# A two-layer decoder trunk on one core: the order of every engine's instructions found with the tile context's other machine model

## The chip, the cores and the metric

The kernel runs on one core of a Trainium2 chip. A core has a matrix engine (TensorE, PE in the profile), three engines for elementwise work (VectorE or DVE, ScalarE or ACT, GpSimd or POOL), a queue engine that here only issues DMAs (SyncE, SP), an on-chip memory (SBUF) and accumulator banks behind the matrix engine (PSUM). The metric is the device time of one execution in microseconds (us), the median of several.

## The reference, cut to what matters

The reference is a trunk of two layers for one sequence of 512 tokens with 1024 features, in fp32. Its loop is

```python
for layer in range(DEPTH):
    g = norm_gains[layer]
    hn = rmsnorm(x, g[0])
    if layer % 2 == 0:
        mix = fox_gdn_mixer(hn, ...)        # forgetting attention (8 heads) | gated DeltaNet (4 heads)
    else:
        mix = hgrn2_mamba2_mixer(hn, ...)   # HGRN2 (4 heads) | Mamba-2 SSD (8 heads)
    x = x + rmsnorm(mix, g[1])
    hn = rmsnorm(x, g[2])
    x = x + rmsnorm(conv_ffn(hn, ...), g[3])
```

Each mixer is one input projection, two kinds of heads side by side, and an output projection. The conv-FFN is an up projection to 2 x 2816 columns, a short causal convolution over the tokens, silu(gate) * up, and a down projection. The recurrences (DeltaNet, HGRN2, SSD) are computed in chunks of 64 or 128 tokens: scores within a chunk, and a state that is carried from chunk to chunk by a scan. The DeltaNet also solves a triangular system in each chunk. The HGRN2 scores need, per feature, products of decays between two tokens.

## The kernel before, in words

All large products are made of three fp32r matmuls: each operand is split into a high and a low part, and hi*hi, hi*lo and lo*hi are summed in PSUM. A weight block is loaded by SP into a tile raw (L183), ACT casts the high part (hi, L186) and DVE subtracts it for the low part (lo, L187). The products have three helpers: feature-major blocks fm (L247 to L249), token-major groups tm (L301 to L303), and the output projections y (L321 to L323). One such matmul has 512 columns; the text calls it a large one. They use four PSUM banks (psA). Everything else on PE, the "side" matmuls of the heads, takes its bank from four others (psB).

Layer 0's mixer has, beside the large products, the attention heads (up to L533) and the DeltaNet: pm (L626) makes the matrices M of the chunks, M goes through DRAM (stored at L630 as dM, loaded at L660 as Ms) into a layout in which DVE inverts blocks of 16 by 15 pairs of small instructions (L671, L672; base16), the results go back through DRAM as dX and dY (L673, L676, loaded at L680, L682), three doubling steps finish the solve (pp L698, pq L705, px L712), and the scan over four chunks follows. A step of the scan is pks (L725) on PE, r on DVE, pu (L731) on PE, u on ACT, pst (L738) on PE and the new state S on DVE; po and pqs (L749, L756) make its output, and pt (L395) transposes it.

Layer 1's mixer runs, beside the large products, four HGRN2 heads. A head (hgrn_head) first makes raw scores pdq (L888), which ACT copies into acc (L890) and POOL masks (L891):

```python
S.copy(A, pdq)
G.tensor_tensor(v4(A), v4(A), bcm(ident, 4), op=ALU.mult)
```

Then it goes through seven block sizes. For each of the first six, DVE subtracts the first halves of a tile Z (L904) and POOL the second halves (L905), ACT takes the exponential (L906), DVE and POOL multiply the halves by k and q (L907, L908), PE makes the products pz (L916) and DVE copies a part of them into acc (L922). The seventh needs one POOL product (L911). POOL also makes el, qg and kd of a head (L927, L930, L934), and PE pk (L938). After the SSD's small columns (L383) a softplus on DVE ends in `a` (L968), and three small matmuls pg (L970 to L972) sum it. The convolution of the SSD's input is four taps on a tile cv, the first on ACT (L343), three on DVE (L345). The SSD block then makes per chunk masks W on DVE (L1020), their products pd (L1021), pcb (L1028, L1029), an exponential, a POOL product LT (L1034), px, pst and py (L1038, L1051, L1062). The scans of HGRN2 (L1097 to L1110) and the transposes for the output projection (L395) follow.

What sets the order: the program's text names, by generators and a table PACE, in which order the instructions are emitted, large products and side streams interleaved. This order is only a priority. At the exit of the tile context a list scheduler plays the whole program on a model of the machine and places, on each engine, at each moment the ready instruction that comes first in priority; tiles wait for free buffers of their pools. What the model says about durations so decides what stands next to what. The kernel is compiled with the order found, and each engine then runs its list strictly in order. The context is opened at the end of the host function:

```python
with tile.TileContext(nc) as tc:
    trunk(tc, *args)
```

Of the kernel before, what the change touches and what calls it, by code (L numbers as in the profile page):

```python
# [16 lines left out]
P = 128  # L17
T = 512
NT = T // P
D = 1024  # L20
# [7 lines left out]
# rounds of the side streams per block of the products they run beside  # L28
PACE = dict(heads=(3, 3, 4, 2), ssd=(0, 2, 1), scan=5, gate=1, fox=(3, 4, 3), pre=2, pre_from=4, base=8, at=8, solve=(1, 1), small=4)
# rows of blocks by which the first token tile of a group runs ahead, and the row before which the other group's norms stand  # L30
LEAD = (3, 3)
NORMS = (1, 4)
# columns of the packed per-feature constants
C_GCONV, C_MCONV, C_MCB, C_FCONV, C_FCB, C_LBL, C_END = 0, 48, 80, 88, 352, 440, 448
# columns of the packed rows
R_FB, R_DTB, R_GAL, R_MDT, R_MAL, R_MD, R_GG, R_HG, R_MG, R_END = 0, 8, 12, 16, 24, 32, 40, 168, 296, 808
# columns of the shape constants
# [4 lines left out]
def trunk(ctx: ExitStack, tc: tile.TileContext, x, gains, w_s, w_a, w_b, w_o, w_u, w_d, gcols, cols, rows, consts, out, taps=None):  # L42
    nc = tc.nc
# [43 lines left out]
    def bc3(col, n, w):  # L87
        """[P, n] -> [P, n, w], each column spread over w"""
        return col.unsqueeze(2).to_broadcast([P, n, w])

    def bcm(m, n):
        """[P, w] -> [P, n, w], the same for each n"""
        return m.unsqueeze(1).to_broadcast([P, n, m.shape[1]])
# [34 lines left out]
    def rsq(out_, in_, n):  # L128
        """out = in ** -0.5"""
        G.tensor_tensor(out_, in_, negh[:, :n], op=ALU.pow)  # L130
# [3 lines left out]
    # 16 matrices [128, 128] each, 128 apart: their 128 diagonal 16 x 16 blocks are evenly spaced  # L134
# [5 lines left out]
    def chunk4(d, n):  # L140
        """[128 rows, 4 matrices, 128 columns] of chunk n"""
# [3 lines left out]
    def diag16(d):  # L145
        """[128, 16, 16]: the 16 x 16 diagonal blocks"""
# [12 lines left out]
    def lockstep(gens):  # L159
        """all advance by one step per round"""  # L160
# [5 lines left out]
    def skewed(gens):  # L166
        """one more starts per round"""
# [29 lines left out]
    def inv_rms(src):  # L197
        """1 / rms of the token tile src (two halves)"""
# [6 lines left out]
        r = tn(1, "r")  # L205
# [3 lines left out]
    def prenorm(t, xt, which, hT, bank):  # L209
        """rmsnorm of the token tile xt (two halves), transposed into hT columns of tile t"""  # L210
# [21 lines left out]
    def postnorm(xt, y, gain):  # L232
        """xt += rmsnorm(y) * gain; y: two banks"""
# [17 lines left out]
    def fm_small(ps, src, hT):  # L251
        """as fm_mm, for up to 16 features: src [128, 8 * 48] holds them twice, from columns 0 and 32.
        Rows 0 of the bank get the products with the weights' upper parts, rows 32 those with the rest."""
# [14 lines left out]
    def fm_blocks(srcs, hT, done, nsplit=0):  # L268
        """feature-major products: one [128 features, 512 tokens] bank each, handed to done(i, bank).
        The first nsplit blocks take the last token tile separately."""  # L270
# [19 lines left out]
    def tm_group(srcs, hT, done, meanwhile=None):  # L290
        """token-major product: 512 features for all the tokens; done(t, bank). meanwhile() after every quarter"""
# [19 lines left out]
    def out_group(srcs, lhs, bank, hooks, lead):  # L311
        """two token tiles times [K, 1024]: lhs(k) -> per token tile (hi, lo); returns banks[tile][half].
        The first tile takes the last lead rows of blocks before the second one does. hooks[k]() before row k"""
# [26 lines left out]
    def conv(ps, taps_, bias, width, slot=slot):  # L340
        """causal depthwise conv along the free axis: taps_ [P, width]; -> slot"""
# [6 lines left out]
    def silu_half(out_, yh, slot=slot):  # L348
        """out = silu(2 yh), by tanh"""
# [4 lines left out]
    def softplus(xs, n, tagp):  # L354
        """softplus of [P, n] (max(x, 0) + log1p(exp(-|x|)), the latter as 2 atanh(u / (2 + u)))"""
# [21 lines left out]
    def small_cols(ps, n, slot=slot):  # L377
        """bank of fm_small -> [128, 4, n] (tokens on partitions)"""
# [12 lines left out]
    def to_mx(src, slot=slot):  # L391
        """token-major [128 tokens, 512] -> split transposed [128, 4, 128]"""
# [7 lines left out]
    # ================= layer 0: FoX | gated DeltaNet =================  # L400
    def mixer0(hT):
        # FoX projections
        # q: its upper part in the rows of its head, the rest in the other head's rows; k: the upper part in both, and the rest
# [44 lines left out]
        # per-token scalars  # L448
# [19 lines left out]
        # -8 * cumsum(log_f), as rows spread over the partitions  # L468
# [892 lines left out]
```

## Time and profile before

| what | value |
|---|---|
| time, median of 3 runs | 1393.02 us (1390.69 to 1393.9) |
| span of the profiled execution, first to last instruction | 1391.2 us |
| the profiled execution's own time | not listed apart from the three above; the median is 1.8 us over its span |
| PE busy | 1343.0 us, 97% of the span, 6836 matmuls |
| DVE, ACT, POOL busy | 893.7 (64%), 664.0 (48%), 151.6 us (11%) |
| mean granted clock of PE | 0.993 of full speed |

The profile is one execution taken by the hardware profiler. A matmul counts as busy from its start to its modelled end, so PE's busy share says where it had work, not that the work ran at its peak. Where an engine was idle, the profile names the instruction that ended the wait. [...]

### The profile page before, as it was taken

How to read it: one execution, taken by the hardware profiler on the slowest of the kernel's cores; microseconds unless marked ns; L12 is line 12 of the kernel's file. 1: busy time of each engine (PE TensorE's matmuls, PEld its weight loads, DVE VectorE, ACT ScalarE, POOL GpSimd, SP SyncE). 2: the span in 40 equal slices, each digit the busy share in tenths (PEclk: the TensorE clock that was granted, in tenths of full speed). 3: DMA queues.
4: the chain of work that ended last, by engine and by line, in shares of the span. 5: the costliest groups of instructions: out<-in, count | busy, mean ns of one | idle time of the engine just before them, and what ended most of it. 6: DMA issues, size and time to landing. Idle time of an engine off the chain costs nothing. (4 is left out here: it accounts for less than half of the span.)

```text
span 1391.2 us, 18400 instructions
## 1 busy us (share of the span) xinstructions
PE 1343.0 (97%) x6836; PEld 1124.6 (81%) x6836; DVE 893.7 (64%) x1616; ACT 664.0 (48%) x1253; POOL 151.6 (11%) x159
## 2 busy tenths in 40 slices
PE   7999999999999999999999879899999999999998
PEld 6877777887988888888888768678888888888886
DVE  5546777667865565556664877876677556555564
ACT  6625644435744434346554534425575443434552
POOL 0000111101000000000010546452010000000000
PEclk9999999999999999999999989999999999999999
DMA  6341123315433333266653212111544323334663
GB/s 227 112 139 59 46 76 61 102 46 176 152 98 105 91 100 98 92 177 201 207 186 97 61 46 77 46 40 55 195 137 123 106 91 100 97 92 149 193 223 117
DMA packets 59418, 159.82 MB, mean 115 GB/s; under 512 B 11968, under 2 KB 18624, under 8 KB 59328
## 3 DMA queue, kind: packets, MB, share of 16 engines
q1 hardware_dynamic: 57600, 156.44, 36.1%
q10 hardware_dynamic: 1728, 2.20, 0.4%
q8 instruction: 54, 0.88, 0.3%
q14 instruction: 36, 0.29, 0.1%
HBM read 151.00 MB, written 7.62 MB: 114 GB/s over the span
## 5 line engine op out<-in xcount | busy, mean ns | idle before, releaser
L187 DVE TENSOR_TENSOR lo<-raw,hi 128x1024 fp32r<-128x1024 f32 x264 | 323.8, 1230 | 333.1 <-ACT hi L186 332.7
L186 ACT CAST hi<-raw 128x1024 fp32r<-128x1024 f32 x264 | 276.6, 1052 | 320.2 <-PE fm L248 130.2
L247 PE MATMUL fm<-hh,hi 128*128 128x512 f32 (+1 forms) x1120 | 411.7, 369 | 2.0 <-ACT hh L229 1.6
L249 PE MATMUL fm<-hh,lo 128*128 128x512 f32 (+1 forms) x1120 | 411.8, 368 | 0.0
L248 PE MATMUL fm<-hl,hi 128*128 128x512 f32 (+1 forms) x1120 | 411.3, 368 | 0.0
L247 PEld LDWEIGHTS fm<-hh,hi 128*128 128x128 f32 x1120 | 212.3, 190 | 37.1 <-ACT hh L229 2.0
L249 PEld LDWEIGHTS fm<-hh,lo 128*128 128x128 f32 x1120 | 212.6, 190 | 34.8 <-issue 1.2
L248 PEld LDWEIGHTS fm<-hl,hi 128*128 128x128 f32 x1120 | 212.6, 190 | 34.5 <-issue 1.4
L321 PE MATMUL y<-hi,ahl 128*128 128x512 f32 x352 | 137.2, 390 | 0.0
L322 PE MATMUL y<-lo,ahl 128*128 128x512 f32 x352 | 136.9, 389 | 0.0
L323 PE MATMUL y<-hi,ahl 128*128 128x512 f32 x352 | 136.6, 389 | 0.0
L345 DVE SCALAR_TENSOR_TENSOR cv<-fm,col,cv 128x511 f32<-128x511 f32 (+1 forms) x176 | 130.8, 746 | 2.8
L130 POOL TENSOR_TENSOR r<-ms,negh 128x1 f32<-128x1 f32 x32 | 21.1, 664 | 820.3 <-DVE ms L204 820.3
L321 PEld LDWEIGHTS y<-hi,ahl 128*128 128x128 f32 x352 | 66.1, 188 | 14.1 <-issue 0.5
L323 PEld LDWEIGHTS y<-hi,ahl 128*128 128x128 f32 x352 | 66.1, 188 | 13.9
L322 PEld LDWEIGHTS y<-lo,ahl 128*128 128x128 f32 x352 | 66.1, 188 | 13.6
L191 ACT CAST ahl<-cv 128x256 fp32r<-128x256 f32 x88 | 34.6, 404 | 83.7 <-DVE cv L1244 83.7
L1240 ACT ACTIVATE cv<-cv 128x512 f32<-128x512 f32 x44 | 27.8, 632 | 84.8 <-DVE cv L345 84.8
L343 ACT ACTIVATE cv<-fm,col 128x512 f32<-128x512 f32 x88 | 68.1, 774 | 0.0
L301 PE MATMUL tm<-hi,hh 128*128 128x512 f32 x160 | 63.8, 398 | 4.4 <-DVE cv L345 4.4
L303 PE MATMUL tm<-hi,hl 128*128 128x512 f32 x160 | 62.9, 395 | 0.0
L302 PE MATMUL tm<-lo,hh 128*128 128x512 f32 x160 | 62.8, 392 | 0.0
(325 smaller groups left out, 1727.0 us busy)
## 6 DMA issues: line engine op xcount, KB each, us to landing
raw<-in_w_u SPq DMA_DIRECT2D x88, 512.0 KB, 3.6
raw<-in_w_d SPq DMA_DIRECT2D x88, 512.0 KB, 4.2
raw<-in_w_o SPq DMA_DIRECT2D x32, 512.0 KB, 3.7
raw<-in_w_a SPq DMA_DIRECT2D x28, 512.0 KB, 3.6
raw<-in_w_b SPq DMA_DIRECT2D x28, 512.0 KB, 3.7
x<-in_x SPq DMA_DIRECT2D x16, 256.0 KB, 4.7
g<-in_gains SPq DMA_DIRECT2D x4, 512.0 KB, 4.5
xs_dram<-x SPq DMA_DIRECT2D x8, 256.0 KB, 2.9
```

Source lines behind the costliest of these rows:

```text
L186: S.copy(hi, raw)
L187: V.tensor_tensor(lo, raw, hi.bitcast(F32), op=ALU.subtract)
L247: PE.matmul(ps[:, a:b], lhsT=wh, rhs=hh[:, a:b], start=(k == 0), stop=False)
L248: PE.matmul(ps[:, a:b], lhsT=wh, rhs=hl[:, a:b], start=False, stop=False)
L249: PE.matmul(ps[:, a:b], lhsT=wl, rhs=hh[:, a:b], start=False, stop=(k == KB - 1))
L301: PE.matmul(banks[t], lhsT=hh[:, a:b], rhs=wh, start=(k == 0), stop=False)
L303: PE.matmul(banks[t], lhsT=hl[:, a:b], rhs=wh, start=False, stop=(k == KB - 1))
L321: PE.matmul(y[j][half], lhsT=ah, rhs=hi[:, c], start=(k == 0), stop=False)
L322: PE.matmul(y[j][half], lhsT=ah, rhs=lo[:, c], start=False, stop=False)
L323: PE.matmul(y[j][half], lhsT=al, rhs=hi[:, c], start=False, stop=(k == n - 1))
L343: S.activation(y, ps, AF.Identity, bias=bias if bias is not None else 0.0, scale=taps_[:, width - 1:width])
L345: V.scalar_tensor_tensor(y[:, s_:], ps[:, :T - s_], taps_[:, width - 1 - s_:width - s_], y[:, s_:], ALU.mult, ALU.add)
```

## The change: the scheduler's machine model

One argument is added where the tile context is opened, so that the scheduler plays the program on the other model that the context offers. The rest of the difference is comments and text strings in functions that were taken out; no instruction is added or taken away on any engine, except that one of ACT's six table loads stands at another line (L925 in place of L906).

```diff
     args.append(nc.dram_tensor("out_0", (T, D), F32, kind="ExternalOutput").ap())
-    with tile.TileContext(nc) as tc:
+    with tile.TileContext(nc, schedule_with_timeline_sim=True) as tc:
         trunk(tc, *args)
```

What moves is the order. In the conv-FFNs it is the same on all engines. It differs in layer 0's mixer (from some 100 to 380 us of the trace of before), in layer 1's mixer and output projection (720 to 1060 us), and by a few rows at the start, the boundaries of the layers and the end. Counted over the program, 2922 rows of difference are on PE, 1412 on DVE, 769 on ACT, 108 on POOL and 84 on SP. Three places follow. A name is a tile and its number, then what it is made from; x4 means four in a row.

On PE, around pg (L970) in layer 1, before; tm are large matmuls of the tokens' products, pz_7389 is the second block size of the second head:

```order
L301 MATMUL tm_7419<-hi_7487,hh_5446 128x512
L302 MATMUL tm_7419<-lo_7488,hh_5446 128x512
L303 MATMUL tm_7419<-hi_7487,hl_5447 128x512
L970 MATMUL pg_7373<-a_7371,kc 128x32
L971 MATMUL pg_7373<-a_7371,kc 128x32
L972 MATMUL pg_7373<-a_7371,kc 128x32
L916 MATMUL pz_7389<-Z_7383 128x128 x4
L916 MATMUL pz_7401<-Z_7395 128x128 x4
```

And the same place in the changed kernel:

```order
L302 MATMUL tm_7419<-lo_7609,hh_5454 128x512
L303 MATMUL tm_7419<-hi_7608,hl_5455 128x512
L301 MATMUL tm_7420<-hi_7608,hh_5454 128x512
L970 MATMUL pg_7373<-a_7371,kc 128x32
L971 MATMUL pg_7373<-a_7371,kc 128x32
L972 MATMUL pg_7373<-a_7371,kc 128x32
L916 MATMUL pz_7389<-Z_7383 128x128 x4
L916 MATMUL pz_7401<-Z_7395 128x128 x4
```

The rows of pg stand behind other large matmuls: the weight hi_7608 is two further on than hi_7487. Counted, 49 more large matmuls stand ahead of pg, and 41 more ahead of the first pz of the first head (pz_7080).

On POOL, the second head of HGRN2, a piece of the difference (- is before, + is the changed kernel); Z_7299, Z_7383 and so on are the block sizes from 64 down, acc_7296 the head's scores:

```order
 L905 TENSOR_TENSOR Z_7299<-G_7014 128x4x64
-L891 TENSOR_TENSOR acc_7296<-acc_7296,kc 128x512
 L905 TENSOR_TENSOR Z_7383<-G_7014 128x8x32
 L905 TENSOR_TENSOR Z_7395<-G_7014 128x16x16
-L908 TENSOR_TENSOR Z_7299<-Z_7299,sg_6833 128x4x64
-L908 TENSOR_TENSOR Z_7383<-Z_7383,sg_6833 128x8x32
 L905 TENSOR_TENSOR Z_7407<-G_7014 128x32x8
 L905 TENSOR_TENSOR Z_7453<-G_7014 128x64x4
 L905 TENSOR_TENSOR Z_7465<-G_7014 128x128x2
 L911 TENSOR_TENSOR Z_7477<-sg_6860,sg_6833 128x512
+L891 TENSOR_TENSOR acc_7296<-acc_7296,kc 128x512
+L927 COPY el_7517<-eg_7515 128x4
```

The mask of the scores (L891) moved from the second place of the head behind all its subtractions (L905) and L911. Heads 1 and 4 have the same move; in head 3 it stands behind three of the six subtractions.

On PE, the scan of the gated DeltaNet in layer 0, from the first pst (L738) on, before; y are large matmuls of the output projection:

```order
L738 MATMUL pst_2968<-u_2963,kd_1503 128x128 x4
L321 MATMUL y_3214<-hi_3218,mxh_2702 128x512
L322 MATMUL y_3214<-lo_3219,mxh_2702 128x512
L323 MATMUL y_3214<-hi_3218,mxl_2703 128x512
L321 MATMUL y_3215<-hi_3218,mxh_2702 128x512
L725 MATMUL pks_2975<-S_2973,qkv_976 128x128
L725 MATMUL pks_2975<-S_2973,qkv_1063 128x128
L725 MATMUL pks_2975<-S_2973,qkv_1171 128x128
L725 MATMUL pks_2975<-S_2973,qkv_1269 128x128
L322 MATMUL y_3215<-lo_3219,mxh_2702 128x512
L323 MATMUL y_3215<-hi_3218,mxl_2703 128x512
L321 MATMUL y_3212<-hi_3236,mxh_2628 128x512
```

And in the changed kernel:

```order
L738 MATMUL pst_2968<-u_2963,kd_1503 128x128 x4
L725 MATMUL pks_2975<-S_2973,qkv_976 128x128
L725 MATMUL pks_2975<-S_2973,qkv_1063 128x128
L725 MATMUL pks_2975<-S_2973,qkv_1171 128x128
L725 MATMUL pks_2975<-S_2973,qkv_1269 128x128
L731 MATMUL pu_2985<-r_2980,Y_2480 128x128 x4
L738 MATMUL pst_2995<-u_2990,kd_1539 128x128
L749 MATMUL po_3005<-u_2963,ET_1723 128x128 x4
L738 MATMUL pst_2995<-u_2990,kd_1539 128x128 x3
L725 MATMUL pks_3030<-S_3000,qkv_976 128x128
L725 MATMUL pks_3030<-S_3000,qkv_1063 128x128
```

The large matmuls that stood between the scan's steps are gone from there: between the first pu and the first pt behind the scan stand 44 large matmuls before and 11 in the changed kernel, all 11 ahead of the first pst.

## Rows read from the trace of the kernel before

**Rows 1.** The page's part 1: busy time, share of the span and instructions of each engine.

```profile
PE 1343.0 (97%) x6836; PEld 1124.6 (81%) x6836; DVE 893.7 (64%) x1616; ACT 664.0 (48%) x1253; POOL 151.6 (11%) x159
```

**Rows 2.** Stretches: from:to, length, busy us of each engine, clock, DMA share, GB/s.

```profile
210.00:280.00 70.00, 65.40 (x428) 56.90 (x427) 48.36 (x116) 28.62 (x76) 9.15 (x8) 1.00 0.32 81
...
420.00:490.00 70.00, 70.00 (x310) 57.98 (x309) 42.08 (x53) 28.38 (x40) 0.00 (x0) 1.00 0.32 98
...
770.00:840.00 70.00, 57.55 (x303) 48.08 (x302) 57.29 (x87) 26.87 (x43) 37.11 (x40) 0.90 0.17 53
840.00:910.00 70.00, 62.99 (x344) 52.90 (x343) 57.79 (x113) 27.69 (x42) 30.77 (x31) 1.00 0.21 61
910.00:980.00 70.00, 66.29 (x384) 56.28 (x383) 51.08 (x103) 32.91 (x87) 30.39 (x26) 1.00 0.16 50
```

**Rows 3.** Waits of PE: line, what it waited for, us in total, times, longest.

```profile
PE pg L970 <- DVE a L968: 6.8, 1, 6.8
PE pz L916 <- POOL Z L908: 4.4, 2, 3.9
PE tm L301 <- DVE cv L345: 4.4, 2, 3.1
...
PE pd L1021 <- DVE W L1020: 2.5, 3, 1.6
```

**Rows 4.** Timeline of PE: start, us, instruction [idle before, what ended it].

```profile
775.95 2.62 PE L916 MATMUL pz<-Z 128*128 128x128 f32 x16 [3.94 <-POOL Z L908]
...
821.43 0.64 PE L970 MATMUL pg<-a,kc 128*128 128x32 f32 x2 [6.81 <-DVE a L968]
...
956.82 0.90 PE L395 MATMUL pt<-kc,y 128*128 128x128 f32 x4 [1.45 <-DVE y L1086]
```

**Rows 5.** Stretches at the lower clock, columns as in rows 2.

```profile
777.26:780.68 3.42, 3.42 (x13) 2.94 (x12) 3.42 (x5) 2.88 (x5) 3.42 (x5) 0.50 0.00 0
...
821.43:828.46 7.03, 7.03 (x33) 7.03 (x34) 1.28 (x4) 0.45 (x2) 0.00 (x0) 0.50 0.21 72
```

**Rows 6.** Timeline of DVE, the instruction that makes `a`.

```profile
821.19 0.19 DVE L968 SCALAR_TENSOR_TENSOR a<-spl,ea 128x32 f32<-128x32 f32 x1
```

**Rows 7.** Waits of POOL.

```profile
POOL acc L891 <- ACT acc L890: 36.3, 3, 16.1
```

**Rows 8.** Timelines of PE and of DVE, the SSD block.

```profile
900.12 0.39 PE L1021 MATMUL pd<-W,sLR 128*128 128x512 f32 x1
...
918.90 0.78 PE L1062 MATMUL py<-X,LT 128*128 128x64 f32 x6
...
894.68 0.84 DVE L1020 TENSOR_SCALAR W<-kc,ahi 128x128 fp32r<-128x128 f32 x4
...
901.79 2.95 DVE L1020 TENSOR_SCALAR W<-kc,ahi 128x128 fp32r<-128x128 f32 x4
```

**Rows 9.** Timeline of PE, layer 0: pm, pp, pu, pt.

```profile
203.62 1.11 PE L626 MATMUL pm<-qkv 128*128 128x128 f32 x8
...
243.83 1.16 PE L698 MATMUL pp<-Y,M 128*128 128x128 f32 x8 [1.58 <-DMA Y<-dY]
...
284.70 1.06 PE L731 MATMUL pu<-vb,Y 128*128 128x128 f32 x8
...
312.86 1.02 PE L395 MATMUL pt<-kc,gg 128*128 128x128 f32 x4 [0.85 <-DVE gg L770]
```

**Rows 10.** Load of Ms on SP, its landing, DVE's first instruction on it.

```profile
208.64 0.36 SPq L660 DMA_DIRECT2D Ms<-dM  x1
...
Ms<-dM SPq DMA_DIRECT2D x1, 128.0 KB, 3.1
...
214.31 0.07 DVE L661 MEMSET Ms<- 128x16 f32 x1
```

**Rows 11.** DVE L904: all by form, and two places of the timeline.

```profile
L904 DVE TENSOR_TENSOR Z<-G 128x256 f32<-128x256 f32 x24 | 20.9, 902 | 0.0
...
848.02 1.09 DVE L904 TENSOR_TENSOR Z<-G 128x256 f32<-128x256 f32 x3
...
866.02 1.46 DVE L904 TENSOR_TENSOR Z<-G 128x256 f32<-128x256 f32 x1
```

## The prediction

> **What bounds the kernel now.** I read the page's busy table first: TensorE (PE) is busy 1343.0 of 1391.2 us, the next engine, VectorE (DVE), 64% [rows 1]. So the end is set by PE, and since the change leaves every instruction on its engine, the time can only move by what PE does not do: idle time and time at the lower clock. The table by 70 us stretches shows where these are. Inside a conv-FFN PE is busy 70.00 of 70 with 310 matmuls, 0.226 us for each large one; short of 70 are 210 to 280 (65.40), 770 to 840 (57.55, mean clock 0.90), 840 to 910 (62.99) and 910 to 980 (66.29) [rows 2]. The first is layer 0's mixer, the other three are layer 1's. The waits say what ended the idle time: one of 6.8 us for `a` (L968), 4.4 us for POOL's Z (L908), 4.4 for the convolution's first tap (L345), 2.5 for W (L1020) [rows 3]. [...]
>
> **What the change moves.** Nothing is added or removed but the place of one table load on ACT. In the two conv-FFNs the order is the same on every engine; at the start, the boundaries and the end matmuls move by a few rows, where PE is busy nearly all the time. I give these parts 0, bounds -1.5 and +1.5. What is left are five places, each costed as: large matmuls that now stand ahead of a point, times 0.226 us, against the time at which its input can be there.
>
> **1. From the first pz to pg (layer 1): -11.** 41 more large matmuls (9.3 us) stand ahead of the first pz, more than its wait of 3.94 [rows 4], so that wait goes. Ahead of pg (L970) stand 49 more, 11.1 us. pg now starts at 821.43, 0.05 us after the instruction that makes `a` ends [rows 4, 6]. The DVE work in front of `a` is nearly the same, and DVE is busy 57.29 of the 70 us [rows 2]; of the 12.7 others 5.75 lie in the 7.03 us behind pg's start [rows 5]. So `a` comes at about the same time, and PE has by then done 11.1 us more. Without a long idle time the half clock behind pg (3.5) goes as well: 14.6 at most. Against it: on DVE the copy of the first pz's result (L922) now stands behind a tap of a convolution, and the third pz must wait for that PSUM bank. Walking both orders with the trace's durations I get a wait of 4 us there and pg at 824 instead of 821.4, and I leave 1 us for a clock that falls after that wait: 14.6 - 2.6 - 1 = 11. Bounds: 7 (`a` 7.6 us later or the clock lost again) and 14.6.
>
> **2. From pg to the last pz: -5.** POOL's mask of the scores (L891) waits for ACT's copy of the same head's pdq. Now it stands second or third in a head's POOL work, and POOL waited there three times, 36.3 us together [rows 7], with five of the six subtractions (L905) or more queued behind it. In the new order of heads 1, 2 and 4 all six and L911 stand ahead of it, in head 3 three of the six. PE's idle time between 840 and 910 is 70 - 62.99 = 7.0 [rows 2], of which some 6 lie before the last pz and are waits for Z or a tap behind Z. I take 5 of them; bounds 0 (DVE's half of Z is late as well) and 6.
>
> **3. The SSD block: +5.** Between the fourth pd (L1021) and the first py (L1062) stand 41 large matmuls now and none after: they are spent earlier, on places 1 and 2. The stretch takes 18.8 us now (900.12 to 918.90) [rows 8]; 41 x 0.226 = 9.3 of it are those matmuls, some 2.5 waits for W [rows 3], so 7 are its own matmuls. What feeds them is a chain: W on DVE, pd, exp, POOL's product, py. The block needs 32 W: at the price of 4 in 0.84 us that is 6.7 us, at 2.95 for 4 (while POOL works) 23.6 [rows 8]. With the other DVE work of the chain I walk 13.5 us, so 6.5 of idle time in place of 2.5: +4, and +1 for the next stretch up to the scan's first pst. Bounds 0 and +9 (18.8 again, less the waits already there, less 7).
>
> **4. The output projection's start: -1.4.** 22 more large matmuls (5 us) stand ahead of the transpose at 956.82 that waits 1.45 us now [rows 4]. Bounds -1.5 and 0.
>
> **5. Gated DeltaNet in layer 0: +4.** Three stretches [rows 9]. From pm (203.62) to the solve's first pp (243.83), 40.2 us, the number of large matmuls falls from 96 to 72, 5.4 us less cover; now 3.9 of the 40.2 are not matmuls, so 36.3 - 5.4 = 30.9 remain. The chain there (pm, M, store, load, base16, store, load) can shrink: the load of Ms was issued at 208.64 and took 3.1, but DVE only came to clear its tile at 214.31 [rows 10], held by a weight's L187 that the new order puts behind; and no weight load stands between the stores of dX and dY on SP any more. I take 36, so 5 us of stall in place of 3.9: +1. From pp to pu (284.70), 40.9 us, 20 large matmuls more (4.5 us) cover small waits: -1.5. From pu to pt (312.86), 28.2 us, the scan keeps 11 of its 44: 33 x 0.226 = 7.5 us less. Its matmuls alone take 28.2 - 2.2 - 7.5 = 18.5; the chain pst, S, pks, r, pu, u cannot run in less than that nor should it need more than 28.2. I take 25, near the upper end, since each of three steps crosses to DVE and ACT and back: 6.5 of stall for 2.2, +4.3. Sum +4; bounds -5 (chains as short as the matmuls: -3.9 - 1.5, nearly all of the idle time now) and +11.5 (both chains as long as now: stalls of 9.3 and 9.7 for 3.9 and 2.2, less 1.5).
>
> **Sum.** -11 - 5 + 5 - 1.4 + 4 = -8.4. Since the walk is by hand I round toward no change: -8. The durations come from one execution with a span of 1391.2 us; its own time isn't among the three shown, whose median is 1393.02, 1.8 above that span. I subtract from the median: 1385.0.
>
> [...] DVE's first half of Z (L904) took 0.36 us each when three ran while POOL waited (848.02, 1.09 for 3), 1.46 for one while POOL worked (866.02), and 902 ns in the mean of 24 [rows 11]. [...]
>
> **The rivals.**
> *Larger gain.* Places 3 and 5 cost nothing, because what feeds them is also earlier: -11 - 5 - 1.4 - 1.5 (pp to pu) = -19: 1374. For it: pz's last matmul would then come some 17 us earlier than now, and DVE isn't busy all the time behind it. Against it: 41 matmuls fewer beside W, 33 fewer beside the scan.
> *No change: DVE sets layer 1's stage.* If all 24 L904 ran at 1.46 instead of 0.902, DVE would need 13.4 us more; if half of that lands ahead of `a` and of the last pz, places 1 and 2 fall from -16 to -9, and with +5, -1.4 and +4 about -1.5 is left: 1391.5, at most 1395. For it: rows 11 and DVE's 57 us of 70. Against it: POOL's work is the same, only less interrupted.
> *Slower: the scan and solve of layer 0 run bare.* If both chains of place 5 stay as long as now, the stage loses 11.5 more than now, and one fall of the clock like that behind pg adds 3.5, together 15. With places 1 to 4 as forecast (-12.4) this gives +2.6: 1395.6; with places 1 and 2 at their low ends (-7, 0) it gives -7 + 5 - 1.4 + 15 = +11.6: 1404.6; between the two, 1400. For it: the order leaves the scan 11 large matmuls. Against it: DVE and SP have less in front of base16. It decides when the stage from 200 to 320 loses more than layer 1 gains: from 12.4 us on with places 1 to 4 as forecast.
>
> **How the numbers follow.** The three times of before span 3.2 us, so 0.2% (2.8 us, below 1390.2 or above 1395.8) is about what can be told from no change. Forecast 0.50 (its own range 1378 to 1390), larger gain 0.14, no change 0.16, slower 0.20. The forecast's upper edge lies at the bound, so nearly all of it counts as faster: faster 0.62, with a little of the forecast in the same: same 0.18, slower 0.20. The range leaves out half of the larger gain and rather more than half of the slower case: 1372 to 1398.
>
> **What would show each step.** In the changed profile: place 1 right if pg waits under 2 us and no half clock follows, wrong if pg's wait is again over 5 us, or starts after 830. Place 2: POOL's wait at L891 far below 36 us, PE's idle time in the heads under 3 us. Place 3: waits of py or pd for W, LT or the like of 6 to 8 us in a row where there were 2.5. Place 5: waits of pks, pu or pst in the scan of some 6 us and of pp for the DMA of 4 to 5. It is wrong as a whole if DVE's mean of L904 rises above 1.2 us with pg late, or if the stage of layer 0 loses over 12 us.

## The result, and the profile after

The changed kernel took 1412.9 us, the median of 4 runs (1409.97 to 1415.96), beside 1393.33 for the kernel before on the same chip: a ratio of 1.0151, 95% interval 1.0131 to 1.0172. It is slower by 1.5%, some 20 us, where 8 us faster was forecast. The profiled execution took 1409.97 us with a span of 1408.2. It is compared below with the profiled span of before, 1391.2: 17.0 us to explain.

The busy table, beside [rows 1]:

```profile
PE 1351.3 (96%) x6836; PEld 1136.3 (81%) x6836; DVE 896.4 (64%) x1616; ACT 663.4 (47%) x1253; POOL 151.2 (11%) x159
```

PE has the same 6836 matmuls and is busy 8.3 us longer, so about half of the loss is no idle time. The table by 70 us stretches (columns as in [rows 2]) shows why: three of six stretches have a mean granted clock below 1.00, which is full speed; in before it was one of these six (770 to 840, 0.90).

```profile
140.00:210.00 70.00, 66.08 (x324) 52.40 (x324) 37.32 (x157) 36.77 (x116) 9.18 (x8) 0.88 0.14 42
210.00:280.00 70.00, 65.94 (x413) 56.14 (x412) 52.40 (x154) 28.44 (x81) 6.61 (x6) 1.00 0.34 89
280.00:350.00 70.00, 62.38 (x400) 54.86 (x399) 43.16 (x94) 28.55 (x83) 10.40 (x9) 1.00 0.19 59
...
770.00:840.00 70.00, 59.80 (x299) 49.19 (x299) 55.95 (x69) 31.48 (x48) 38.93 (x37) 0.95 0.20 62
840.00:910.00 70.00, 65.58 (x381) 56.77 (x380) 59.99 (x106) 27.46 (x43) 30.37 (x31) 1.00 0.21 62
910.00:980.00 70.00, 61.19 (x340) 52.80 (x339) 45.84 (x113) 24.84 (x69) 31.05 (x26) 0.93 0.12 38
```

The waits of PE, beside [rows 3]:

```profile
PE pz L916 <- DVE acc L922: 10.0, 2, 8.3
PE pd L1021 <- DVE W L1020: 8.0, 4, 3.9
...
PE tm L301 <- DVE cv L345: 3.8, 2, 2.2
PE pt L395 <- DVE gg L770: 2.6, 1, 2.6
...
PE pu L731 <- DVE r L728: 2.0, 3, 1.1
...
PE pt L520 <- ACT s L516: 1.4, 2, 1.1
```

The wait of pg for `a` and that of pz for POOL's Z are gone, as forecast. A wait of pz for its bank (8.3) and the waits for W (8.0) have taken their place. The timeline of PE at the points of [rows 4] and [rows 9]:

```profile
223.53 0.33 PE L626 MATMUL pm<-qkv 128*128 128x128 f32 x1
...
257.57 0.27 PE L698 MATMUL pp<-Y,M 128*128 128x128 f32 x1
...
302.07 0.28 PE L731 MATMUL pu<-vb,Y 128*128 128x128 f32 x1
...
331.56 0.30 PE L395 MATMUL pt<-kc,gg 128*128 128x128 f32 x1 [2.57 <-DVE gg L770]
...
815.34 2.05 PE L916 MATMUL pz<-Z 128*128 128x128 f32 x8 [8.35 <-DVE acc L922]
...
850.36 0.30 PE L970 MATMUL pg<-a,kc 128*128 128x32 f32 x2
```

How a loss is read from such starts: pm begins 19.9 us later than in [rows 9] (223.53 against 203.62). 37 large matmuls more stand ahead of it, 37 x 0.226 = 8.4 us of work that isn't lost but done earlier. So 11.5 us are lost by then. The same sum at each point gives this account, where a place's loss is the difference between the sums at its two ends; both a lower clock and idle time are in it. "Small" stands from here on for PE's side matmuls, though some of them have 512 columns too.

| place | forecast | loss (+) or gain (-) |
|---|---|---|
| start, attention heads, up to pm of layer 0 | 0 | +11.5 |
| 5: pm to pu | -0.5 | -1.6 |
| 5: the scan, pu to pt | +4.3 | +8.8 |
| pt to layer 1's first pdq | 0 | +1.7 |
| 1: first pdq to pg, with the half clock behind pg | -11 | -6.1 |
| 2: pg to the last pz, without that half clock | -5 | -1.6 |
| 3: SSD block, to the scan's pst | +5 | +10.5 |
| 4: output projection's start | -1.4 | -1.6 |
| output projection and boundary behind it | 0 | -4.9 |
| sum (in the prediction -8.4, with place 5 rounded) | -8.6 | +16.7 |

Two of the smaller rows hold a half clock that one trace has and the other lacks. The first of these two stretches, all at 0.50, is from after: its 3.42 us of matmuls at half speed cost 1.7, the +1.7 of the fourth row. The second is from before and is in the -4.9 (number 12).

```profile
371.22:374.64 3.42, 3.42 (x17) 3.42 (x18) 3.42 (x9) 2.29 (x8) 0.54 (x1) 0.50 0.99 311
...
1012.78:1016.19 3.41, 3.41 (x15) 2.92 (x14) 2.62 (x7) 1.25 (x4) 0.00 (x0) 0.50 0.74 229
```

The largest term is at a place that the prediction gave 0 without looking into it. All of it is lost behind the twelfth of the attention's 32 scores (L504; 157.43 in after, 135.27 in before): up to there the sum is -0.2. The stretches from this score to pm (columns as in [rows 2]):

```profile
157.43:166.43 9.00, 7.89 (x44) 5.49 (x42) 5.18 (x24) 4.85 (x13) 1.27 (x1) 1.00 0.20 58
166.43:183.49 17.06, 16.04 (x54) 12.87 (x54) 11.36 (x53) 9.87 (x39) 3.30 (x3) 0.50 0.01 1
183.49:223.53 40.04, 37.47 (x212) 29.61 (x210) 24.48 (x95) 22.03 (x65) 4.58 (x4) 1.00 0.15 46
```

For 17.06 us the granted clock stood at 0.50, and PE was busy 16.04 of them: at half speed these cost 8.0 us. Idle times, the longest 1.11 us, make 4.7 more. Together that is a little over the 11.5, so the split is an estimate. In before, the same attention work, from its twelfth score to pm, ran at the full clock throughout:

```profile
134.90:203.60 68.70, 68.52 (x370) 53.10 (x369) 47.89 (x188) 40.53 (x124) 9.19 (x8) 1.00 0.18 55
```

Counted by their starts, 136 of the 367 matmuls between the two points are large in before and 74 of 305 in the changed kernel; the 231 small ones are the same. From 157.43 to 183.49, where the clock fell, 11 large ones start, 9 of them at its end. What PE did just before the fall, in its timeline:

```profile
163.33 0.42 PE L504 MATMUL ps<-fqk,fqk 128*128 128x384 f32 x1
163.69 0.44 PE L505 MATMUL ps<-fkl,fqk 64*128 64x384 f32 x1
165.23 0.72 PE L520 MATMUL pt<-kc,s 128*128 128x128 f32 x3 [1.11 <-ACT s L516]
165.71 0.48 PE L504 MATMUL ps<-fqk,fqk 128*128 128x512 f32 x1
166.12 0.55 PE L505 MATMUL ps<-fkl,fqk 64*128 64x512 f32 x1
```

These are small matmuls alone, with one idle time of 1.11 us. Before the halves of [rows 5] PE had been idle for 3.94 and 6.81 us [rows 4]; here it had not.

### The profile page after: what moved, and what is told of

The parts are those of the page before. It is cut to its first block, busy times and chain, and to the rows that moved or that the text cites. A ratio compares the mean times of both kernels' runs of the same rounds, so it can differ in the third digit from the quotient of the medians.

```text
span 1408.2 us, 18404 instructions
## 1 busy us (share of the span) xinstructions
PE 1351.3 (96%) x6836; PEld 1136.3 (81%) x6836; DVE 896.4 (64%) x1616; ACT 663.4 (47%) x1253; POOL 151.2 (11%) x159
## 4 chain that ended last, share of the span: by engine, by line
PE 84%; DVE 8%; ACT 3%; DMA 2%; issue 1%; POOL 1%; SPq 0%; DVEq 0%; POOLq 0%; ACTq 0%
PE fm L247 15%; PE fm L248 15%; PE fm L249 15%; PE y L321 7%; PE y L322 7%; PE y L323 7%; PE tm L301 2%; PE tm L302 2%; PE tm L303 2%; DVE lo L187 1%; DVE Z L904 1%; PE po L528 1%; PE pz L916 1%; DVE cv L345 1%; DVE Z L907 1%
## 5 line engine op out<-in xcount | busy, mean ns | idle before, releaser
L247 PE MATMUL fm<-hh,hi 128*128 128x512 f32 (+1 forms) x1120 | 406.6, 370 | 4.0 <-ACT hh L229 2.4
L323 PE MATMUL y<-hi,ahl 128*128 128x512 f32 x352 | 137.1, 389 | 0.0
L321 PE MATMUL y<-hi,ahl 128*128 128x512 f32 x352 | 125.9, 389 | 0.0
L301 PE MATMUL tm<-hi,hh 128*128 128x512 f32 x160 | 63.6, 399 | 3.8 <-DVE cv L345 3.8
```

Of the source, the lines that this page charges most:

```text
L247: PE.matmul(ps[:, a:b], lhsT=wh, rhs=hh[:, a:b], start=(k == 0), stop=False)
L301: PE.matmul(banks[t], lhsT=hh[:, a:b], rhs=wh, start=(k == 0), stop=False)
L321: PE.matmul(y[j][half], lhsT=ah, rhs=hi[:, c], start=(k == 0), stop=False)
L323: PE.matmul(y[j][half], lhsT=al, rhs=hi[:, c], start=False, stop=(k == n - 1))
```

## The experiments

Most of them impose an order: each engine's instructions are chained in the order of a table, on top of the dependences that the program has, so that parts of the two orders can be joined. A cut by a time means the time at which an instruction started in the trace of the kernel that its order is taken from.

```diff
+    traced = [i for i in nc.cur_bb.bb.instructions if type(i).__name__ != "BassTilePoolBoundary"]
...
+        for step in d:
+            k += step
+            if last is not None:
+                tc.add_manual_dep(traced[k], last, mybir.DependencyInfo(mybir.DependencyClass.NoSync, mybir.DependencyReason.DATA), reason="order")
+            last = traced[k].name
...
         trunk(tc, *args)
+        impose(tc, nc, ORDER)
```

The edits below give the table ORDER in words. Imposing an order costs nothing that the traces show: where number 9 has the order of before, pg starts at 821.67 (821.43 in before), and where number 10 has that of after, pm starts at 223.87 (223.53 in after). Each ratio is to the kernel before on the same chip: 1390.82 us beside numbers 1 to 4, 1391.26 beside 5, 9, 10 and 11, 1391.22 beside 6, 8 and 12, 1390.61 beside 7.

The theory was that the loss is layer 0's mixer's, by large matmuls spent early; the rivals, that layer 1 loses, that the loss is one of engines other than PE, or that it is passed on from stage to stage.

**1. Layer 0 in the order of before, the rest in that of after.**

```diff
-ORDER = after
+ORDER = before until 480 us, then after
```

> Every engine's order is that of before up to the middle of layer 0's conv-FFN and that of the change from there on. Theory A (the time is lost in layer 0's mixer, 11.5 us in the attention heads, 8.8 in the DeltaNet scan; layer 1 is 4 us faster than before, because its gains in the heads and behind the scan outweigh the SSD block): about 1389 to 1390, 3 to 4 us under before. Rival B (layer 1's new waits, the 8.35 us at the fifth pz and 7.4 us at the SSD's pd, are the loss, and layer 0's lag would have been absorbed): 1405 or more.

Measured: 1389.95 us beside 1390.82, ratio 0.9994 (0.9985 to 1.0003). The whole loss is gone with layer 0's order, 1.0151 - 0.9994 = 1.6% or 22 us. Layer 1's new order, which the prediction credited with 12.4 us, is worth next to nothing as a whole.

**2. The reverse: layer 0 in the order of after, layer 1 in that of before.**

```diff
-ORDER = after
+ORDER = after until 500 us, then before
```

> The counterpart: the changed order up to the middle of layer 0's conv-FFN, the order of before from there on. Theory A: about 20 us over before, 1413 to 1414, as slow as the whole change or a little slower. Rival B: 1396 or less.

Measured: 1416.57, ratio 1.0182 (1.0167 to 1.0197), 2.6 us over the forecast and far from the rival. The loss is layer 0's.

**3. Only the attention and the start in the order of after.**

```diff
-ORDER = after
+ORDER = after until 246.9 us, then before
```

> The changed order only through the attention heads up to the solve's first products (where both orders have done the same work on PE), the order of before from there on. If the loss of 11 us that the trace shows by then is carried to the end, and the scan is a second, separate loss: 1403 to 1405. If the later lag in the scan follows from the attention's lag (same cause): 1410 or more. If the loss is regained behind it: 1396 or less.

Measured: 1409.38, ratio 1.0132 (1.0115 to 1.0149), which is in none of the three intervals: over the first, just under the second. By starts 11.6 us are lost at pm, as in after. Another 6.9 go between pm and pp, at the seam of the two orders: a wait of 5.78 us of tm (L301) for the tap, ended at 253.42, and a half clock from 251.9 to 258.7, in which the large matmuls of 253.98 to 256.97 start 0.43 us apart; at the full clock ahead of the wait it is 0.23. From there on nothing more is lost: 18.5 at pp, 18.3 at pu and at pt. So the seam spoils the total; the attention's part shows in the trace as in after, and a scan in the order of before loses nothing even when it is reached 18 us late.

**4. Large matmuls put into the bare attention stretch, in addition.** 33 copies of a large matmul without use, 7.5 us, stand ahead of the scores and sums of heads 2 to 4.

```diff
+EXTRA = {(2, 3): 3, (3, "pb"): 3, (3, 0): 3, (3, 1): 3, (3, 2): 3, (3, 3): 6, (4, "pb"): 3, (4, 0): 3, (4, 1): 3, (4, 2): 3}
...
             ps = bankB("ps")
+            for _ in range(EXTRA.get((h, Q), 0)):
+                idle.append(PE.matmul(ps, lhsT=hT[0][0][:, 0:P], rhs=hT[0][0], start=True, stop=True))
```

> The changed kernel with the same order, and 33 more large matmuls (7.5 us at full clock) put between the attention's small ones in the stretch where the changed order has none; what they write is overwritten by the matmul behind them, so the result does not depend on them. Theory C (8.5 of the 11.5 us are TensorE's half clock, which came because the stretch held only small matmuls): no or much less half clock there, and although PE does 7.5 us more, the time is that of the changed kernel or below, 1407 to 1413. Rival D (the chain through DVE and ACT sets this stretch, the clock falls whatever PE does): 1418 to 1421, the clock at half as long as now.

Measured: 1420.38, ratio 1.0217 (1.0198 to 1.0236), 7.5 us over after (9 by the two ratios): the added work was paid in full, as the rival had it. The half clock did not stay as long as the rival had it: the clock fell 10.4 us later and stood at 0.50 for 13.65 us instead of 17.06:

```profile
157.36:176.85 19.49, 17.41 (x94) 12.52 (x92) 9.35 (x47) 10.71 (x42) 2.90 (x3) 1.00 0.10 27
176.85:190.50 13.65, 13.45 (x37) 10.02 (x38) 7.18 (x30) 4.60 (x12) 1.68 (x2) 0.50 0.01 2
```

The price was not even. Below are the same six small matmuls in after and in this kernel, where the copies are L493 and L509 and po is L534:

```profile
171.40 1.38 PE L528 MATMUL po<-fv,pT 128*128 128x64 f32 x6
...
173.01 0.78 PE L534 MATMUL po<-fv,pT 128*128 128x64 f32 x6
174.99 0.96 PE L493 MATMUL pb<-hh 128*128 128x512 f32 x3 [1.20 <-ACT kd L614]
...
177.81 1.63 PE L509 MATMUL ps<-hh 128*128 128x512 f32 x3
```

21 of the copies, 4.7 us of work, stand ahead of that point, and it came only 1.6 us later (173.01 against 171.40): after had been at half clock since 166.43, this kernel still ran at the full one. Then 5.3 us passed without a copy, the clock fell behind three more, and the last nine ran at half.

**5. 24 large matmuls of the same block moved into the bare stretch.** One stands behind every third small one, and the block's weight halves are made later.

```diff
-L248 MATMUL fm_2092<-hl_96,hi_2095 128x512
-L249 MATMUL fm_2092<-hh_95,lo_2096 128x512
...
 L504 MATMUL ps_1323<-fqk_598,fqk_461 128x512
 L505 MATMUL ps_1323<-fkl_601,fqk_461 128x512
+L247 MATMUL fm_2092<-hh_95,hi_2095 128x512
 L520 MATMUL pt_1334<-kc,s_1306 128x128 x3
+L248 MATMUL fm_2092<-hl_96,hi_2095 128x512
```

> The changed kernel with 24 large matmuls (one block, 5.4 us) moved on PE from just ahead of the attention's bare stretch into it, one behind every third small matmul, and the next weight's split (one ACT and one DVE row) behind the stretch; no work is added. Theory C (the bare stretch costs by its half clock, 8.5 us, and by idle time): 4 to 10 us under the changed kernel, 1403 to 1409, with less than 7 us at half clock there. Rival D (the chain of the attention through DVE and ACT sets the stretch): no change, 1411 to 1415, or slower, with idle time where the 24 stood.

Measured: 1412.26, ratio 1.0143 (1.0126 to 1.0161): no better than after, and in the rival's interval. With 96 large matmuls between the twelfth score and pm instead of 74, 13.8 us are lost at pm (225.78). The clock was at half for 17.0 us again, in two other places, both with PE busy all the time. Idle times of 0.99 and 1.40 us had come ahead of the two falls:

```profile
154.75 0.55 PE L520 MATMUL pt<-kc,s 128*128 128x128 f32 x3 [0.99 <-ACT s L516]
...
155.20:162.00 6.80, 6.80 (x25) 5.12 (x24) 0.18 (x1) 2.36 (x5) 1.27 (x1) 0.50 0.00 0
...
174.38 0.44 PE L520 MATMUL pt<-kc,s 128*128 128x128 f32 x2 [1.40 <-ACT kd L608]
...
175.70:185.90 10.20, 10.20 (x28) 7.73 (x29) 7.97 (x30) 3.43 (x8) 1.27 (x1) 0.50 0.09 13
```

One block spread thin did not restore the clock. Numbers 4 and 5 left open whether the lack of large matmuls is the cause at all, or the order on ACT and DVE; numbers 6 and 7 were made for that.

**6. The attention alone in the order of before.**

```diff
-ORDER = after
+ORDER = before until 203.6 us, then after
```

> The order of before up to the first pm (203.6 us), the order of after from there. Theory A (the attention stretch and the scan of layer 0 each lose by their own order, 11.5 and 8.8 us in the trace of after): the 11.5 go, the scan's loss stays: 1412.9 - 11.5 = 1401, between 1398 and 1404 with what the seam costs or saves. Rival S (the scan loses because it is reached late, with other buffers still full from the attention): the scan's loss goes too, 1390 to 1395. In the trace A wants 29 us or more from pu to pt, S 28.2 - 7.5 = 21.

Measured: 1400.83 beside 1391.22, ratio 1.0064 (1.0050 to 1.0078). 0.87% or 12.1 us of after's loss are gone, the 11.5 of the account. From the twelfth score to pm PE had 76.72 us of work in 76.89 at full clock:

```profile
134.69:211.58 76.89, 76.72 (x405) 59.85 (x404) 49.13 (x189) 41.54 (x125) 9.19 (x8) 1.00 0.19 59
```

The scan still took 29.48 us (pu 293.50, pt 322.98), as in after. It loses by its own order, not because it is reached late.

**7. Only the spending: the order of after up to the attention's twelfth score, then that of before on all engines.**

```diff
-ORDER = after
+ORDER = after until 157.4 us, then before
```

> The order of after up to 157.4 us of its trace (the attention's first scores), with its 99 matmuls more ahead of that point; from there the order of before on every engine, in which no large matmul is left between the first scores and the first pm (26 in after, 78 in before). Theory P (the attention loses because its large matmuls were spent ahead of it): the stretch from the scores to pm stays near the 60 us that are left of the 66.1 in after without its 26 large matmuls, the clock falls to half for 10 us or more, pm comes at 215 to 220, and the time is 1399 to 1407. Rival E (it loses because ACT and DVE do the attention's own instructions in a poorer order): the stretch takes about the 51 us that are left of before's 68.7 without its 78, pm comes by 211, the clock stays, and the time is 1390 to 1395.

Two corrections to that text: 157.4 us is the start of the twelfth score, not of the first, which starts at 102.18; and its counts of 26 and 78 large matmuls end at the first pm of another chunk. Up to the pm of [rows 9] they are 74 in after, 136 in before and 37 in this kernel. Measured: 1408.18 beside 1390.61, ratio 1.0125 (1.0108 to 1.0143), 1.2 us above the first theory's interval and far from the rival. pm came at 221.60 (1.6 later than expected), with 18.0 us lost, more than in after, although ACT and DVE do the attention in the order of before. The clock was at half for 23.9 and 6.8 us:

```profile
163.65:187.54 23.89, 22.69 (x80) 17.10 (x80) 14.33 (x75) 15.25 (x61) 3.31 (x3) 0.50 0.00 1
187.54:197.78 10.24, 7.54 (x45) 5.38 (x43) 8.25 (x37) 6.43 (x23) 3.30 (x3) 1.00 0.09 26
197.78:204.61 6.83, 6.37 (x16) 4.37 (x17) 4.09 (x14) 2.99 (x9) 0.00 (x0) 0.50 0.09 5
```

With 136, 74 and 37 large matmuls beside the same small ones, 0, 17.1 and 30.7 us stood at half clock, and 0, 11.5 and 18.0 us were lost. The cover that PE spent ahead of the twelfth score is the cause; a poorer order on ACT and DVE is not needed for it. That the number alone decides is not shown: with 96 (number 5) more was lost than with 74.

**8. Only the scan of layer 0 in the order of after.**

```diff
-ORDER = before
+ORDER = before until 284.6 us, after until 331.4 us, then before
```

> The order of after from the first pu to the first pt of layer 0's scan alone; before it and behind it the order of before. Large matmuls that after has ahead of the scan come first in this stretch. Theory A (the scan left with 11 large matmuls of 44 loses by itself): 1393.3 + 8.8 = 1402, between 1399 and 1404. Rival S (the scan loses only behind the attention's delay): 1391 to 1395.

Measured: 1401.29, ratio 1.0072 (1.0058 to 1.0085), 10.0 us. By starts 9.6 us are lost between pu (291.71) and pt (322.05); up to 1.7 of them are a half clock from 312.21 to 315.62 that the scan of after does not have. With number 6 the two parts add up: 12.1 + 10.0 = 22.1 us, number 1 had 22. The agreement to 0.1 us is in part luck: the seams and that half clock are in these numbers. How the bare scan runs, one step of it in the timeline of after:

```profile
307.31 1.16 PE L725 MATMUL pks<-S,qkv 128*128 128x128 f32 x8 [0.78 <-DVE S L741]
308.91 1.26 PE L731 MATMUL pu<-r,Y 128*128 128x128 f32 x8 [0.45 <-DVE r L728]
310.53 0.49 PE L738 MATMUL pst<-u,kd 128*128 128x128 f32 x2 [0.35 <-ACT u L734]
310.86 1.06 PE L749 MATMUL po<-u,ET 128*128 128x128 f32 x8
311.75 0.83 PE L738 MATMUL pst<-u,kd 128*128 128x128 f32 x6
313.02 1.26 PE L725 MATMUL pks<-S,qkv 128*128 128x128 f32 x8 [0.44 <-DVE S L744]
```

A step takes 313.02 - 307.31 = 5.7 us, with many short waits of 0.35 to 1.1 us and the last one of 2.57 for gg. From pu to pt PE is busy for 21.87 of 29.49 us there, at the full clock.

**9. Only the SSD block of layer 1 in the order of after.**

```diff
-ORDER = before
+ORDER = before until 892.5 us, after until 964 us, then before
```

> The order of before everywhere but in the SSD block (from the last pz to the scan's first pst), where it is that of the change: there 52 of the large matmuls stand ahead of the fourth pd and none beside the chain of W, pd, exp, LT and py. If this order alone costs what the changed kernel loses there: 10 us over before, 1400 to 1403, with waits of pd for W and a half clock. Rival (it costs only because the stage arrives there earlier than DVE): 1394 or less.

Measured: 1400.34 beside 1391.26, ratio 1.0064 (1.0049 to 1.0079). As expected, place 3 by itself costs 9 us: waits for W of 3.88 and 3.44 us, and 10.2 us at half clock behind them (914.3 to 921.1, 924.5 to 927.9).

**10. The bank wait of place 1 removed in after.** The four copies on DVE that free pz's banks stand ahead of the taps.

```diff
+L922 COPY_PREDICATED acc_7071<-kc,pz_7080 128x4x64
+L922 COPY_PREDICATED acc_7071<-kc,pz_7092 128x8x32
 L345 SCALAR_TENSOR_TENSOR cv_7057<-fm_7026,mh,cv_7057 128x509
...
-L922 COPY_PREDICATED acc_7071<-kc,pz_7080 128x4x64
 L345 SCALAR_TENSOR_TENSOR cv_7205<-fm_7174,mh,cv_7205 128x510
-L922 COPY_PREDICATED acc_7071<-kc,pz_7092 128x8x32
```

> The changed kernel with four DVE rows moved: the copies of the first four pz (L922) stand ahead of three groups of convolution taps and two of L187 instead of behind them, so that the fifth pz finds a free PSUM bank. If that wait (8.35 us) and the half clock behind it (6.8 us at half speed, 3.4 lost) are the place's cost: 8 to 12 us under the changed kernel, 1401 to 1405. If DVE sets the stage and the wait only goes elsewhere (the taps and with them pg or the second head's pz come as much later): 1409 to 1413.

Measured: 1410.11, ratio 1.0139 (1.0118 to 1.0160): the same as after within the intervals. The wait of 8.35 us is gone, and one of 6.46 stands a little later, in front of the next head's pdq, from 812.61 to 819.07, with 6.8 us at half clock around its end as in after. By starts 2.3 us of the 8.35 are gained up to pg. The rest agrees with the second expectation, that DVE sets this stretch: what is taken from one of its consumers another one waits for.

**11. The parts that gain, joined.** Layer 0 and the SSD block in the order of before, the heads of layer 1 and all behind the SSD block in that of after.

```diff
-ORDER = before
+ORDER = before until 480, after until 904.5, before until 940.8 us, then after
```

> A mixture by places: the order of before up to layer 0's conv-FFN, that of the change through layer 1's HGRN2 heads up to the last pz, that of before through the SSD block up to the scan's first pst, that of the change behind it. If the gains and losses that the trace shows place by place belong to the places (heads -8, SSD block +11 or 0, output projection -6): 13 us under before, about 1377 to 1381. Rival (the SSD block's loss is the price of the heads' gain, since the large matmuls are spent): 1388 to 1392, as fast as before.

Measured: 1383.24 beside 1391.26, ratio 0.9943 (0.9928 to 0.9958): 8 us faster than before, the fastest version of this study, but 2 us above the expected interval.

**12. Only what lies behind the SSD block in the order of after.**

```diff
-ORDER = before
+ORDER = before until 940.8 us, then after
```

> The order of before up to 940.8 us, which is behind the SSD block, and the order of after from there: scan of layer 1, output projection, the last FFN. Theory B (the gain of the mixed order came from behind the SSD block, 6.5 us by places in its trace, whatever the heads do): 1393.3 - 6.5 = 1387, between 1384.5 and 1389. Rival H (the gain needs the heads in the order of after, which end 4.4 us earlier by places; behind the SSD block it only shows): 1391 to 1394.

Measured: 1385.57 beside 1391.22, ratio 0.9959 (0.9947 to 0.9971). 5.7 of the 8 us are there, as expected. PE has 66.66 us of work in 66.84 from the first pt of the output projection to the boundary's transposes:

```profile
958.46:1025.30 66.84, 66.66 (x363) 57.43 (x362) 50.74 (x84) 45.22 (x94) 6.88 (x10) 1.00 0.59 187
```

In before the same stretch had a wait of 1.94 us of pt (L222) for xn, ended at 1011.60, and then 3.4 us at half clock. The half clock was that one execution's: the traces of numbers 2, 3, 7, 8 and 9, which have the order of before there, show the wait with 1.0 to 1.7 us and no half clock behind it, and from the pt of [rows 4] (956.82) to the end they take 1.7 to 2.4 us less than that of before. So about 2 of the -4.9 in the account are not the order's, and about 3 are.

## Why the prediction was wrong

**The boundary of what was costed: the step that failed.** The prediction said that "at the start, the boundaries and the end matmuls move by a few rows, where PE is busy nearly all the time", gave them 0 with bounds of -1.5 and +1.5, and let layer 0's account begin at pm. The attention heads between 100 and 203 us fell through: 99 more large matmuls (22.4 us) stand ahead of the attention's twelfth score in the new order. That PE is busy nearly all the time there in before says that its small matmuls were covered, not that they don't need the cover. The account and number 6 show this term at +11.5 to +12, over half of the loss, and number 7, with 18.0, that the early spending alone brings a loss of this kind.

**Place 5, the scan: mis-sized.** The sign was right, +4.3 forecast, +8.8 in after's trace, +9.6 in the trace of number 8, up to 1.7 of it clock. The step was "the chain ... cannot run in less than that nor should it need more than 28.2. I take 25". Without the large matmuls it took 29.5, 1.3 more than with them, so even the upper bound was too low. From pm to pu -1.6 was measured for -0.5: -0.8 up to pp, where +1 was forecast, and -0.9 behind it for -1.5.

**Place 1: the gain went to a new wait.** The wait that was named, the third pz for a bank that DVE's copy frees, came (as that of the fifth pz), but took 8.35 us where 4 were walked. The clock then fell as feared; its row:

```profile
811.54:818.37 6.83, 3.03 (x13) 2.97 (x14) 6.73 (x11) 1.76 (x3) 2.09 (x1) 0.50 0.25 79
```

PE has only 3.03 us of matmuls in it, so the half clock costs 1.5, where 1 was left for it. DVE is busy 6.73 of the 6.83 us. pg itself no longer waits: `a` was done at 845.7, pg started at 850.36. The half clock behind pg, 7.03 us at 0.50 in [rows 5] and so 3.5 us of cost by estimate, is gone with the wait: from 840 to 910 the mean clock is 1.00. That the clock holds where there is no long idle time was the author's estimate, and the attention does not bear it out: there it fell behind 1.11 us. So of the 11 us, 6.1 came; 4.35 of the 4.9 missing are the longer bank wait. By number 10 the wait isn't the bank's alone, since DVE has the work anyway.

**Place 2: -1.6 instead of -5, and the reason was wrong.** POOL's wait at the mask (L891) did not shrink from the 36.3 us of [rows 7]. Two rows of after, POOL's wait and DVE's L904 by form in layer 1's heads, the latter beside [rows 11]:

```profile
L891 POOL TENSOR_TENSOR acc<-acc,kc 128x512 f32<-128x512 f32 x4 | 5.4, 1357 | 34.9 <-PE tm L302 22.0 <-ACT acc L890 12.9
...
L904 DVE TENSOR_TENSOR Z<-G 128x256 f32<-128x256 f32 x24 | 18.7, 831 | 0.0
```

34.9 us are still there. POOL reaches the mask later, and what it waits for is later too. PE's idle time between pg and the last pz went from 6.1 to 4.4 us. Even the -1.6 is hardly clear of chance: numbers 2, 3, 7, 8 and 12, which have the order of before there, differ from before's trace by -1.5 to +1.3 us over this place.

**L904 on DVE.** By the prediction, a mean of L904 over 1.2 us with pg late would have shown it wrong as a whole, and the rival "DVE sets layer 1's stage" was priced with 1.46 us for each L904. The mean fell from 902 to 831 ns, so neither is what happened.

**Place 3: twice the size.** +5 was forecast with bounds 0 and +9, +10.5 measured, about 9 by number 9. The waits for W came as named, 8.0 us in place of 2.5, where 6.5 were walked. What was left out is the clock behind them:

```profile
931.01:934.42 3.41, 3.11 (x12) 2.75 (x12) 1.53 (x7) 0.93 (x2) 0.46 (x1) 0.50 0.00 0
937.84:944.66 6.82, 6.50 (x20) 5.07 (x20) 4.53 (x17) 0.97 (x2) 2.37 (x2) 0.50 0.01 2
```

These 9.61 us of matmuls at half speed cost 4.8.

**Place 4 and the boundary behind.** -1.6 for -1.4. The -4.9 behind it was not foreseen: the wait of 1.94 us that ended at 1011.60 and the 3.4 us at half clock behind it are gone, which together makes 3.6. By number 12 about 2 of the 4.9 are before's one execution and not the order.

**The rivals.** "The scan and solve of layer 0 run bare" was the nearest, with 1404.6 at its worst, but its stage began at pm too. The point that it gave, "from 12.4 us on", was passed: layer 0 lost 18.7 up to pt. "Larger gain" and "DVE sets layer 1's stage" did not occur, though number 10 shows DVE setting a part of place 1. In the walk of places 1 and 3 the clock was charged once or not at all, while three places (attention, bank wait, SSD) ran 16.04 + 3.03 + 9.61 = 28.7 us of matmuls at half in after, 14.3 us of time; the half clock at 371.22 costs 1.7 more. In before, the halves of [rows 5] cost 5.2 and that at 1012.78 1.7. The difference, 9.1 us, is about the 8.3 us by which PE is busy longer.

**What stays open.** How many large matmuls the attention needs, and where, to keep the clock: 74 were too few, 136 enough, and neither a thin spread of 24 inside the stretch (number 5) nor 33 unused ones (number 4) helped. So it is not shown which part of the 11.5 us the clock costs by itself and which the chain through DVE and ACT. No run has PE's order alone or that of the other engines alone; number 7 replaces it by a cut in time.

## What to carry to other kernels

Where a scheduler moves large matmuls forward, don't look only at the waits that they fill: ask which stretch they are taken from, and cost that stretch as its small matmuls alone, with the waits between them and a half clock (here 17 to 31 of 64 to 66 us). A stretch in which PE is busy all the time in the old order is easily left out, because nothing in its profile shows a wait; here it cost most. Orders can be joined by stages: the parts of two orders that gain were found by cutting each at a few times, and together they beat both.

## What the runs showed that was not expected

- TensorE's clock fell to half without a long idle time. In after 1.11 us was the longest idle time ahead of the fall at 166.4, in a run of small matmuls with PE busy 16.04 of the 17.06 us that followed; in number 5 PE was busy for 6.80 of 6.80 and 10.20 of 10.20 us at a granted clock of 0.50. In the halves of before in [rows 5] an idle time of 3.94 or 6.81 us had come first, in the one at 1012.78 one of 1.94.
- Of 33 unused large matmuls put between the small ones, the first 21 cost 1.6 us instead of 4.7, because the clock of after had fallen to half by then and theirs had not. The fall came 10.4 us later, in a part with few of them, and in the end the 33 cost their 7.5 us in full (number 4).
- A chain from engine to engine that seemed to be covered by matmuls (the scan, 28.2 us) took 29.5 us when 33 of them, 7.5 us, were taken out of it, at the full clock: nearly all of the time between its points was already the chain's.
